# A hybrid GLA and Fourier layer on one core: modulation loads issued by GpSimd, folds a step further ahead, no VectorE modulation in the output gates

## The chip, the cores and the metric

The kernel runs on one core of one Trainium2 chip. The metric is the device time of one execution in microseconds, as the median of several runs. The core has five engines that work in parallel, each through its own list of instructions: PE (TensorE, matrix products), ACT (ScalarE), DVE (VectorE), POOL (GpSimd) and SP (SyncE, which here only issues transfers). Semaphores order the engines against each other. Transfers between the chip's memory and the core run on 16 DMA engines.

## What is computed

The reference is one layer of a diffusion backbone for 128 context tokens and 256 latent tokens, with 2048 channels. It is applied to both sets, which share all weights. Cut to what matters here:

```
mod = silu(cond) @ w_ada + b_ada            # 6 x 2048 values for each of 2 conditions
sh1, sc1, ga1, sh2, sc2, ga2 = split(mod, 6)
h = rmsnorm(x) * (1 + sc1) + sh1
q, k, v, g, lr_f, lr_b, fo = split(h @ w_in)
o = gla(q, k, v, decays) ; o = rmsnorm(o) * silu(g)
f = real(fft2(fo))                          # over positions and over 256 channels of a group
g_a, g_b = split(sigmoid(h @ w_gate + b_gate))
m = (g_a * (o @ w_br_gla) + g_b * (f @ w_br_four)) @ w_out
x = x + ga1 * rmsnorm(m)
h = rmsnorm(x) * (1 + sc2) + sh2
x = x + ga2 * rmsnorm((silu(h @ w_ffn_gate) * (h @ w_ffn_up)) @ w_ffn_down)
```

Everything is in float32. The modulation is a product of a 2048 x 12288 matrix with only two vectors, and its six parts of 2048 are wanted at different times: the first two at the start, the third (ga1, m = 2) in the output projection, the fourth and fifth (m = 3 and 4) before the feed-forward part, the last one at the end.

## The kernel before

**Data.** The 384 tokens lie along the free axis, channels along the 128 partitions. A float32 product is made of three matrix products of halves: each operand is split into a high and a low part (`hi`, `lo`), and hi x hi, hi x lo and lo x hi are summed (`gemm`, L311 to L317). A weight arrives as a tile `raw` of 128 x 1024; ACT copies its high part (L275, L281) and DVE subtracts it for the low part (L276, L282). All weights are listed in the order of use in `srcs` (L158 to L214). `load` (L218) takes the next one with a transfer issued by SP, `split` makes the two parts, and `grab` hands out the next finished pair and pushes another one in, so that about three pairs stand ready. `proj` (L335) makes 128 output channels ("a unit") from h in two half units of 24 matmuls each, and after each half unit calls `step(side)`, which advances a generator of side work by one step. The orders of PE, ACT, DVE and POOL are those in which the program writes its instructions; SP's order is made by a scheduler.

**Modulation.** There are two ways to sum a half of one part (16 tiles of 128 x 1024, 512 KB each). `ada_gemv` (L685) has PE do it: one load (L690) and eight small matmuls (L692; printed as one line of x8) at each step. `ada_rest` (L661) has DVE do it: one load (L666) and two DVE operations (L669 for the first tile, L671 for the others) at each step, then eight matmuls with a selecting matrix (L679) that bring the sums together. Both end in `ada_tail` (L643): ACT copies the sum (L645), PE transposes it (L649), DVE adds the bias and writes `mods`. All loads share two buffers, `adaw`. DVE's sums run through `paced` (L344), which advances them by `rate` steps for each step of the side work and carries fractions over.

**Stages.** After the start (norm, first modulation, values of the GLA) the program goes through these, and PE's own products set the order in each:

- The GLA stage, with the q and k units, then GF = 26 units of the merge gates. Their side work (L939) advances the scan of the GLA, `gl`, by one step, and one step of modulation: in a cycle of seven, PE's sums (`summed`) at the second and fifth, DVE's (`ada`) at the others. A finished gate is written to memory by SP (`gates_d`, L954).
- The fold stage, with the remaining gate units in `turns` half units. The Fourier transform over positions uses that cosines are even and sines odd, so h is first folded over the positions: `over_ends` (L700; DVE L702, L707, L708 and ACT L703) adds and subtracts mirrored positions, `over_parts` (L710) splits the result into `hF` (ACT L356, DVE L357), and `across_n` (L981) makes the product of hF with folded weights into four sums (PE L993, L994). The weights of these products are folded too (`fold_across`, DVE L248 and L249). What is done after each half unit is in the table `after` (L166 to L173): `("ends", n)`, `("parts", n)` and `("f", h, n)` for n from 0 to 7, and h from 0 to 1 for the two halves of the Fourier columns. `run_after` (L1003) goes through it. Three spare buffers for raw weights are in use in this stage. It ends with a small product for the Nyquist columns (`pfq`, L1031).
- The output gates and the branches (`mix_order`): eight units of the GLA's output gate with side work of `summed`, `df` (the transform over positions, L1065) and `ada` at rate 0.5, and after each `next(nw)`, which builds small Nyquist weights `wn` from eight transfers of 12 KB (`nyq_weights`, L1114); between them, from the third on, the Fourier units, `four` (L1181), and then the GLA branch units.
- The output projection, `wout` (L1269 on), 16 units, with `ada` at rate 0.8. After unit i = KT - 4 = 12 everything that `ada_gen` still has is drained in one go, since its buffers are needed. Each unit ends in ACT squares (L1266) and DVE sums (L1277, L1281).
- The feed-forward part, which the change leaves as it is.

The pacing and the drain read:

```
def paced(gen, rate):
    due = 0.0
    while True:
        due += rate[0]
        while due >= 1.0:
            due -= 1.0
            if next(gen, 1) is not None:
                return
        yield
...
            if i == KT - 4:
                for _ in ada_gen:
                    pass
```

Of the kernel before, what the change touches and what calls it, by code (L numbers as in the profile page):

```python
# [35 lines left out]
NFC = FT // FC  # L36
G = 1024
XU = 2
GF = 26
BF = 10  # L40
GD = 256

# [65 lines left out]
def tile_step(ctx: ExitStack, tc: tile.TileContext, a, o):  # L108
    nc = tc.nc
    PE, ACT, DVE, POOL, SP = nc.tensor, nc.scalar, nc.vector, nc.gpsimd, nc.sync  # L110
# [54 lines left out]

    turns = 2 * (32 - GF)  # L166
    after = [[] for _ in range(turns)]
    for n in range(8):
        after[n].append(("ends", n))
        after[n + 1] += [("f", 0, n), ("parts", n + 1)]  # L170
    left = turns - 9
    for n in range(8):
        after[9 + n * left // 8].append(("f", 1, n))  # L173
    across = set()
    for at, todo in enumerate(after):
        srcs.append(a["w_gate"][GF + at // 2, at % 2])
# [484 lines left out]
    def ada_rest(todo):  # L661
        for m, half in todo:
            acc = adap.tile([P, 2, 1024], F32, tag="adacc", name="adacc")
            for k in range(KT):
                w = adap.tile([P, 1024], F32, tag="adaw", name="adaw", bufs=2)
                SP.dma_start(w, a["w_ada"][m - 2, half, k])  # L666
                for c in range(2):
                    if k == 0:
                        DVE.tensor_scalar_mul(acc[:, c, :], w, spad[:, k, c : c + 1])  # L669
                    else:  # L670
                        DVE.scalar_tensor_tensor(  # L671
                            acc[:, c, :], w, spad[:, k, c : c + 1], acc[:, c, :], op0=ALU.mult, op1=ALU.add,
                        )
                yield
            yield
            pr = pss.tile([P, 256], F32, tag="side", name="pr")
            for c in range(2):
                for j in range(4):
                    PE.matmul(  # L679
                        pr[32 * j : 32 * j + 32, :], selr[:, 32 * c : 32 * c + 32],  # L680
                        acc[:, c, j * 256 : (j + 1) * 256], start=c == 0, stop=c == 1,
                    )
            yield from ada_tail(pr, m, half)

    def ada_gemv(m, half):  # L685

        pr = pss.tile([P, 256], F32, tag="side", name="pr")
        for k in range(KT):
            w = adap.tile([P, 1024], F32, tag="adaw", name="adaw", bufs=2)
            SP.dma_start(w, a["w_ada"][m - 2, half, k])  # L690
            for j in range(4):
                PE.matmul(  # L692
                    pr[32 * j : 32 * j + 32, :], spad[:, k, :], w[:, j * 256 : (j + 1) * 256],
                    start=k == 0, stop=k == KT - 1,
                )
            yield
        yield from ada_tail(pr, m, half)
# [12 lines left out]
    def over_parts(k, r):  # L710

        x = hF[k // 4]
        split_act(*(x[:, k % 4 : k % 4 + 2, n, :] for n in range(2)), r)
# [9 lines left out]
    rate = [1.0]  # L723
    ada_gen = ada_rest([(m, half) for m in (2, 3) for half in range(2)])
    ada = paced(ada_gen, rate)
    with ExitStack() as s:
# [209 lines left out]
        gl = gla()  # L936
        summed = ada_gemv(4, 0)

        def side():  # L939
            while True:  # L940
                for n in range(7):
                    next(gl, None)
                    next(summed if n % 3 == 1 and n < 6 else ada, None)
                    yield

        sd = side()
        for i in qk_order[1:]:
# [17 lines left out]
    parts = ((0, HT, 0), (HT, T, HT + HL))  # L965
    fs = ctx.enter_context(ExitStack())
    px = fs.enter_context(tc.tile_pool(name="px", bufs=1))
    with ExitStack() as s:
# [5 lines left out]
        sums, folds = [], {}  # L974
# [28 lines left out]
        def run_after():  # L1003
            for at, todo in enumerate(after):
                for what, *n in todo:
                    if what == "ends":
                        ends(*n)
                    elif what == "parts":
                        if n[0] in folds:
                            over_parts(2 * n[0], folds.pop(n[0]))  # L1010
                    else:
                        if n[0] == 0 and n[1] in folds:
                            over_parts(2 * n[1], folds.pop(n[1]))
                        if n == [1, 5]:
                            depth[0] = 2
                            spare_raws.clear()
                        across_n(*n)
                yield
# [21 lines left out]
    with ExitStack() as s:  # L1040
# [73 lines left out]
        def nyq_weights():  # L1114

            n = D // 2
            for h in range(2):
                wr = pc.tile([P, n], F32, name="wr")
                POOL.memset(wr, 0.0)
                for g in range(4):  # L1120
                    src = a["w_br_four"][8 * h : 8 * h + 8, 32 * g : 32 * g + 1, (2 * g + 1) * P : (2 * g + 2) * P]
                    SP.dma_start(
                        wr[g : g + 65 : 32, :].rearrange("p (i c) -> p i c", c=P),
                        src.rearrange("i p c -> p i c").to_broadcast([3, 8, P]),
                    )
                    if g % 2:
                        yield
                w = wn[:, n * h : n * h + n]
                ACT.copy(w, wr)
                DVE.tensor_sub(w[32:64], wr[32:64], w[32:64].bitcast(F32))  # L1130
                yield

        df = dft()

        summed = ada_gemv(4, 1)
        rate[0] = 0.5

        def side():
            while True:
                next(summed, None)  # L1140
                next(df, None)
                next(ada, None)
                yield

        sd = side()
        nw = nyq_weights()
        oT = alloc_r("B", "o")

        def gcol(p, i):
# [60 lines left out]
        for b, i in mix_order:  # L1210
            if b == "o":
                if i == 1:
                    gate_of()
                proj(psm, hT, lambda p: gcol(p, i), sd)
                next(nw, None)
                if i == 1:
                    gate_of()
                continue
            if b == "b":
                for g in (df, nw):  # L1220
                    for _ in g:
                        pass
                next(summed, None)
                four(i)
            else:
                if mT is None:
                    mT = alloc_A()
                p = psm.tile([P, T], F32, tag="mm", name="pmm")
                gemm(p, grab(hold=True), oT, 8)
                g, y = gates.pop((b, i))  # L1230
                DVE.tensor_mul(g, g, p)
                DVE.tensor_add(y, y, g)
                settle()
# [13 lines left out]
    with ExitStack() as s:  # L1247
# [42 lines left out]
            ACT.activation(sq2, mg32(i), AF.Square)  # L1290
            return sq0, pr, sq2

        rate[0] = 0.8
        spare_h = {-4: ((pe, "hid_hi", 1), (pe, "hid_lo", 1)), -2: ((pe, "S0", 1), (pe, "S1", 1))}
        spare_w = ((adap, "adaw", 2), (adap, "adaw", 2))
        raw2 = None
        for i in range(KT):
            p = psm.tile([P, T], F32, tag="mm", name="pmm")
            for g in range(2):
                n = 2 * i + g - 2 * KT  # L1300
                if n < -6:
                    w = grab()
                else:

                    w = take()
# [376 lines left out]
        n = 0  # L1682
# [353 lines left out]
```

## Time and profile before

| | us |
|---|---|
| median of 3 runs | 2013.39 (2011.44 to 2013.53) |
| the profiled execution, device time | 2014.74 |
| its span in the trace | 2012.9 |
| mean granted TensorE clock | 0.988 |

The profile is of one execution. A row of the timeline has the start, the length, the engine, the line of the kernel, the operation, its output and inputs, sizes and a count; what stands in square brackets is the idle time of the engine before it and what ended it. Groups by line have count, busy time, mean ns of one and idle time before. A window's row sums the busy time of each engine in a stretch of time. In the wait view a row reads: engine, instruction, what released it, then the sum of the waits in us, how many, and the longest. The stages of the trace are: start to 147, GLA stage from there to 468, fold stage to 584, output gates and branches to 817, wout to about 952, feed-forward to the end.

### The profile page before, as it was taken

Reading aid. Unit: us, or ns where it says so; the run is one execution under the profiler, and the core shown is the slowest. Engines: PE = TensorE matmul, PEld = TensorE weight load, DVE = VectorE, ACT = ScalarE, POOL = GpSimd, SP = SyncE. Lnnn points to the kernel's source line nnn. Section 1 sums busy time; section 2 is a strip of 40 time slices with the busy share of each in tenths; the row PEclk is TensorE's granted clock in tenths of the full one; section 3 lists DMA queues with packets and bytes.
Section 4 is the critical chain, followed back from the end, with each engine's and each line's share of the span. In section 5 each row is a group of like instructions: output and inputs, shape, how many; then the busy total and the mean of one; then the engine's idle time right before and its main releaser. Section 6 shows DMA issues by size and latency. Waiting matters only on the chain.

```text
span 2012.9 us, 27779 instructions
## 1 busy us (share of the span) xinstructions
PE 1955.7 (97%) x10678; PEld 1709.9 (85%) x10678; DVE 1602.1 (80%) x2128; ACT 915.7 (45%) x1298; POOL 33.2 (2%) x55
## 2 busy tenths in 40 slices
PE   8998999997898899999999999999999999999998
PEld 6778999997897799999988888888888888888886
DVE  5666767677755778896878988999999889987886
ACT  4234454543344465445645444444444444444445
POOL 0000000000000000000300000000000000000001
PEclk9998999999899899999999999999999999999999
DMA  9976767775355778665627363635455354626244
GB/s 390 381 248 201 255 202 232 243 225 189 123 175 167 247 240 264 218 200 178 215 84 222 103 204 94 205 118 181 133 176 165 128 185 129 197 87 192 73 143 151
DMA packets 200597, 380.55 MB, mean 189 GB/s; under 512 B 14092, under 2 KB 126924, under 8 KB 196112
## 3 DMA queue, kind: packets, MB, share of 16 engines
q1 hardware_dynamic: 199936, 378.51, 57.7%
q8 instruction: 84, 1.38, 0.3%
q14 instruction: 49, 0.40, 0.1%
q10 hardware_dynamic: 528, 0.26, 0.0%
HBM read 361.94 MB, written 16.78 MB: 188 GB/s over the span
## 4 chain that ended last, share of the span: by engine, by line
PE 70%; DVE 3%; DMA 2%; ACT 1%; issue 1%; POOL 0%; DVEq 0%; ACTq 0%; POOLq 0%
PE pgu L327 29%; PE pdn L327 17%; PE pmm L315 16%; PE pf L1191 2%; PE pfo L993 1%; PE pmm L1453 1%; PE pf L1192 1%; DMA adaw<-in_w_ada 1%; PE ptr L1745 1%; PE pr L692 1%; PE pfo L994 0%; DMA raw<-in_w_d 0%; DVE x1b L1897 0%; DVE wlo L1611 0%; ACT hF L356 0%
## 5 line engine op out<-in xcount | busy, mean ns | idle before, releaser
L315 PE MATMUL pmm<-A_hi,whi 128*128 128x384 f32 x1072 | 365.1, 341 | 0.0
L315 PE MATMUL pmm<-A_lo,whi 128*128 128x384 f32 x1072 | 360.1, 336 | 0.0
L315 PE MATMUL pmm<-A_hi,wlo 128*128 128x384 f32 x1072 | 360.0, 336 | 0.0
L1600 ACT CAST whi<-u 128x1024 fp32r<-128x1024 f32 x200 | 210.6, 1053 | 273.3 <-DVE u L1584 86.2
L276 DVE TENSOR_TENSOR wlo<-raw,whi 128x1024 fp32r<-128x1024 f32 x163 | 198.6, 1221 | 103.5 <-ACT whi L275 102.1
L1600 ACT CAST whi<-raw 128x1024 fp32r<-128x1024 f32 x175 | 184.2, 1053 | 211.2 <-DMA raw<-in_w_g 69.6
L1611 DVE TENSOR_TENSOR wlo<-u,whi 128x1024 fp32r<-128x1024 f32 x200 | 243.8, 1219 | 28.7 <-ACT whi L1600 18.7
L327 PE MATMUL pgu<-whi,A_hi 128*128 128x512 f32 x640 | 250.0, 391 | 0.0
L327 PE MATMUL pgu<-whi,A_lo 128*128 128x512 f32 x640 | 249.3, 389 | 0.0
L275 ACT CAST whi<-raw 128x1024 fp32r<-128x1024 f32 x165 | 172.9, 1050 | 149.7 <-DMA raw<-in_w_out 65.0
L1611 DVE TENSOR_TENSOR wlo<-raw,whi 128x1024 fp32r<-128x1024 f32 x175 | 213.3, 1219 | 34.4 <-ACT whi L1600 24.8
L315 PEld LDWEIGHTS pmm<-A_hi,whi 128*128 128x128 f32 x1072 | 202.6, 189 | 10.9 <-issue 9.3
L315 PEld LDWEIGHTS pmm<-A_lo,whi 128*128 128x128 f32 x1072 | 202.7, 189 | 0.2
L315 PEld LDWEIGHTS pmm<-A_hi,wlo 128*128 128x128 f32 x1072 | 202.4, 189 | 0.0
L327 PE MATMUL pdn<-whi,hid_hi 128*128 128x512 f32 x480 | 187.0, 390 | 1.1 <-ACT psums L1760 1.1
L327 PE MATMUL pdn<-whi,hid_lo 128*128 128x512 f32 x480 | 186.8, 389 | 0.0
L327 PE MATMUL pgu<-wlo,A_hi 128*128 128x512 f32 x640 | 184.2, 389 | 0.0
L671 DVE SCALAR_TENSOR_TENSOR adacc<-adaw,spad,adacc 128x1024 f32<-128x1024 f32 x120 | 148.5, 1278 | 0.8 <-DMA adaw<-in_w_ada 0.7
L327 PEld LDWEIGHTS pgu<-whi,A_hi 128*128 128x128 f32 x640 | 120.1, 188 | 26.1 <-issue 0.8
L327 PEld LDWEIGHTS pgu<-wlo,A_hi 128*128 128x128 f32 x640 | 120.2, 188 | 25.4
L327 PEld LDWEIGHTS pgu<-whi,A_lo 128*128 128x128 f32 x640 | 120.2, 188 | 25.0
L327 PE MATMUL pgu<-whi,S 128*128 128x512 f32 x480 | 131.1, 395 | 0.0
(402 smaller groups left out, 3019.9 us busy)
## 6 DMA issues: line engine op xcount, KB each, us to landing
adaw<-in_w_ada SPq DMA_DIRECT2D x96, 512.0 KB, 4.3
raw<-in_w_d SPq DMA_DIRECT2D x88, 512.0 KB, 4.1
slab<-in_w_ada SPq DMA_DIRECT2D x32, 1024.0 KB, 10.6
raw<-in_w_gate SPq DMA_DIRECT2D x64, 512.0 KB, 4.6
raw<-in_w_g SPq DMA_DIRECT2D x48, 512.0 KB, 4.1
raw<-in_w_u SPq DMA_DIRECT2D x48, 512.0 KB, 3.7
raw<-in_w_in SPq DMA_DIRECT2D x44, 512.0 KB, 4.7
u<-in_w_u SPq DMA_DIRECT2D x40, 512.0 KB, 4.6
```

The source lines that it names most:

```text
L275: ACT.copy(hi, raw)
L276: sub = lambda: eng.tensor_sub(lo, raw, hi.bitcast(F32))
L315: PE.matmul(dst, w[wi][:, k * n + n0 : k * n + n0 + P], x[xi][:, k0 + k, :], start=first and k == 0 and j == 0, stop=last and k == kts - 1 ...
L327: PE.matmul(dst, stat[x_][m], mov(w[w_], m), start=first and w_ == m == x_ == 0, stop=last and w_ == m == 1,)
L671: DVE.scalar_tensor_tensor(acc[:, c, :], w, spad[:, k, c : c + 1], acc[:, c, :], op0=ALU.mult, op1=ALU.add,)
L692: PE.matmul(pr[32 * j : 32 * j + 32, :], spad[:, k, :], w[:, j * 256 : (j + 1) * 256], start=k == 0, stop=k == KT - 1,)
L993: PE.matmul(p, w_of[0][:, i, k, g, :], x[:, :, lo:hi], start=kt == 0, stop=False)
L1191: PE.matmul(pf[:, 0 : 2 * HT], w[0][:, c], x[k], start=k == 0, stop=False)
L1192: PE.matmul(pf[:, 0:HT], w[1][:, c], x[k][:, 0:HT], start=False, stop=m == 1 and k == 3)
L1453: PE.matmul(hp[u], hw[u][j][:, ((k - 1) % 8) * P : ((k - 1) % 8 + 1) * P], h2[m][:, k - 1, :], start=k == 1 and j == m == 0, stop=k == KT ...
L1600: ACT.copy(hi, src)
L1611: DVE.tensor_sub(lo, src, hi.bitcast(F32))
```

## The change

Seven edits, all in the stages from the GLA to wout:

- the loads of both modulation sums and the eight Nyquist loads are issued by POOL instead of SP;
- GF is 25 instead of 26, so that one more gate unit, two half units, stands in the fold stage (14 turns instead of 12);
- in the table of the fold stage, the split of a fold (`parts`) and its product (`f`) stand one and two turns behind the fold (`ends`), at the head of their turn, where the product stood one turn behind, with the split directly before it; the second half's products begin at turn 10 and spread over the turns that are left;
- in the GLA stage PE's modulation sums stand at the third and sixth step of each cycle of seven, in every cycle, and the cycle is counted through;
- in the output gates the side work has no `ada` step any more, and the Nyquist weights' steps move into it, from once a unit to once a half unit;
- rate 0.5 for the output gates falls away, and the rate in wout is 0.82 instead of 0.8;
- in the Nyquist weights, the two yields stand behind the four loads instead of between them.

```diff
-GF = 26
+GF = 25
...
-        after[n + 1] += [("f", 0, n), ("parts", n + 1)]
-    left = turns - 9
+        after[n + 1].insert(0, ("parts", n))
+        after[n + 2].insert(0, ("f", 0, n))
     for n in range(8):
-        after[9 + n * left // 8].append(("f", 1, n))
+        after[10 + n * (turns - 10) // 8].append(("f", 1, n))
...
                 w = adap.tile([P, 1024], F32, tag="adaw", name="adaw", bufs=2)
-                SP.dma_start(w, a["w_ada"][m - 2, half, k])
+                POOL.dma_start(w, a["w_ada"][m - 2, half, k])
...
         def side():
+            n = 0
             while True:
-                for n in range(7):
-                    next(gl, None)
-                    next(summed if n % 3 == 1 and n < 6 else ada, None)
-                    yield
+                next(gl, None)
+                next(summed if n % 7 in (2, 5) else ada, None)
+                n += 1
+                yield
...
                     elif what == "parts":
-                        if n[0] in folds:
-                            over_parts(2 * n[0], folds.pop(n[0]))
+                        over_parts(2 * n[0], folds.pop(n[0]))
                     else:
-                        if n[0] == 0 and n[1] in folds:
-                            over_parts(2 * n[1], folds.pop(n[1]))
...
-                    SP.dma_start(
+                    POOL.dma_start(
                         wr[g : g + 65 : 32, :].rearrange("p (i c) -> p i c", c=P),
                         src.rearrange("i p c -> p i c").to_broadcast([3, 8, P]),
                     )
-                    if g % 2:
-                        yield
+                yield
+                yield
...
         summed = ada_gemv(4, 1)
-        rate[0] = 0.5
+        nw = nyq_weights()
 
         def side():
             while True:
                 next(summed, None)
                 next(df, None)
-                next(ada, None)
+                next(nw, None)
                 yield
...
                 proj(psm, hT, lambda p: gcol(p, i), sd)
-                next(nw, None)
...
-        rate[0] = 0.8
+        rate[0] = 0.82
```

The load of `ada_gemv` changes in the same way as the one shown.

More of the change, by code (lines that the diff above doesn't have):

```diff
@@ L689, in ada_gemv @@
             w = adap.tile([P, 1024], F32, tag="adaw", name="adaw", bufs=2)
-            SP.dma_start(w, a["w_ada"][m - 2, half, k])
+            POOL.dma_start(w, a["w_ada"][m - 2, half, k])
             for j in range(4):
@@ L1141, in side @@
                 next(df, None)
-                next(ada, None)
+                next(nw, None)
                 yield
         sd = side()
-        nw = nyq_weights()
         oT = alloc_r("B", "o")
```

## The prediction

> **What bounds the kernel now.** I read the page's head and its table of DMA issues, then the windows by stage, then the waits of PE and SP.
>
> ```profile
> span 2012.9 us, 27779 instructions
> PE 1955.7 (97%) x10678; PEld 1709.9 (85%) x10678; DVE 1602.1 (80%) x2128; ACT 915.7 (45%) x1298; POOL 33.2 (2%) x55
> adaw<-in_w_ada SPq DMA_DIRECT2D x96, 512.0 KB, 4.3
> ```
>
> TensorE is busy for 97% of the span: a change can win only part of the 57 us in which PE idles, and it loses whatever new idling it makes. The span lies within a profiled execution of 2014.74 us. The 96 transfers of the last row (4.3 us from issue to landing) are the modulation loads that move from SP to GpSimd; how long one takes there is the first unknown, L below. The windows are the start of the GLA stage, the fold stage, most of the output-gate stage, and wout up to its modulation's end (columns: window and length, then busy time and count of PE, PEld, DVE, ACT, POOL, then the granted clock, the DMA share and GB/s):
>
> ```profile
> 147.00:219.00 72.00, 65.64 (x400) 62.05 (x400) 52.23 (x65) 29.79 (x44) 0.62 (x2) 0.93 0.66 218
> 474.00:584.50 110.50, 91.89 (x574) 88.07 (x573) 78.08 (x114) 44.51 (x74) 0.24 (x2) 0.92 0.47 152
> 632.00:726.00 94.00, 81.70 (x506) 74.25 (x503) 62.58 (x113) 45.38 (x65) 0.96 (x1) 0.89 0.64 209
> 817.00:940.00 123.00, 123.00 (x722) 122.10 (x721) 104.86 (x129) 59.38 (x97) 0.00 (x0) 1.00 0.62 204
> ```
>
> PE idles 6.4 us in the first, 18.6 in the fold stage, 12.3 in the output gates, nothing in wout. In wout the clock is full and PE never waits, but DVE is busy for 104.86 of 123 us: there is nothing to win there, and little room.
>
> ```profile
> PE pr L692 <- DMA adaw<-in_w_ada: 17.2, 5, 5.3
> PE pfo L993 <- DVE hF L357: 16.1, 7, 8.8
> SPq L666 <- DVE adacc L671: 108.3, 36, 9.4
> ```
>
> Two waits make most of PE's idle time: 17.2 us in five waits for modulation loads, 16.1 in seven for folds of h. SP's 108.3 us behind DVE look larger, but they lie where PE is full (wout is one such place), so moving them off SP's queue is worth nothing there.
>
> **The change part by part. Wout: loads that arrive too late to be spread.** Without the output gates' share, wout must sum 23 modulation loads on DVE where it summed 16. Rate 0.82 brings 19 of them up to unit 12; in the built order the last four stand in one burst, and directly behind them, before unit 13's matmuls, PE has L679, which waits for the burst.
>
> ```profile
> 895.31 0.49 ACT L1266 ACTIVATE sq<-pmm 128x384 f32<-128x384 f32 x1
> 900.97 2.47 DVE L671 SCALAR_TENSOR_TENSOR adacc<-adaw,spad,adacc 128x1024 f32<-128x1024 f32 x2
> 919.39 0.49 ACT L1266 ACTIVATE sq<-pmm 128x384 f32<-128x384 f32 x1 [0.34 <-PE pmm L315]
> 905.35 1.07 PE L679 MATMUL pr<-adacc,selr 128*32 128x256 f32 x16
> 909.15 0.36 ACT L645 COPY adev<-pr 128x256 f32<-128x256 f32 x1
> 463.16 0.38 PE L649 MATMUL ptm<-ident,adev 128*128 128x128 f32 x2
> 650.09 1.08 PE L692 MATMUL pr<-adaw,spad 128*32 128x256 f32 x8 [3.93 <-DMA adaw<-in_w_ada]
> 655.64 0.64 PE L692 MATMUL pr<-adaw,spad 128*32 128x256 f32 x8
> 651.10 0.69 PE L1191 MATMUL pf<-edT,whi 128*128 128x388 f32 x1
> 656.21 0.45 PE L1191 MATMUL pf<-edT,whi 128*128 128x388 f32 x1
> 658.71 0.36 PE L315 MATMUL pmm<-A_hi,whi 128*128 128x384 f32 x1
> ```
>
> Seven more loads are 7 x 2.47 = 17.3 us of DVE: 104.9 + 17.3 = 122 of 123. DVE therefore runs late up to unit 12, as it already did at unit 9, where the modulation pair ends at 903.44, 8.1 us after the square that its unit's matmuls released (895.31). So, with T the end of unit 12's matmuls (about 919.1), the last paced pair ends at T + 8.1, the first pair of the burst (its load is there) at T + 10.5. Only two buffers exist: the load of the second was let go at T + 8.1, lands at 8.1 + L and is summed by 10.5 + L; the third rides beside it; the fourth's goes out when the second is summed, and ends at 12.9 + 2L. Then L679 (1.07 hot; 2.1 at the slow clock that follows idling), the copy and its handoff 0.7, the transposes 0.5, and a slow first stretch. That stretch is 2.0 us: a Fourier unit took 4.54 us (651.10 to 655.64) straight after a stall and 2.50 (656.21 to 658.71) later. The 1.4 us of these that PE paid before, without waiting, come off: a loss of 16.8 + 2L. Nothing hides it: all matmuls behind L679 wait in PE's order.
>
> **How long a load takes from GpSimd.** No row of before shows one.
>
> ```profile
> DMA to landing us min/median/max: 3.5/4.0/5.2
> raw<-in_w_v SPq DMA_DIRECT2D x16, 512.0 KB, 6.7
> ```
>
> The first row (loads of L690) gives 3.5 as the lower bound, the second, the same size amid a loaded start, 6.7 as the upper. I take 5.3, next to the slowest of L690's (5.2) and one microsecond over the 4.3 of the ninety-six: the queue is another, untried in this trace, and an issue that GpSimd has to work for is likelier to add time than to save it. The loss in wout is then 27.4 us (23.8 to 30.2).
>
> By the Trainium skill (DMA: Bandwidth & Descriptors, "Anatomy of one DMA — SWDGE (gpsimd) path") a GpSimd transfer takes about 2.0 us plus its bytes at 436 GB/s; that is an estimate of 3.2 us here, below every row of SP, and the loss would be 23.2. No run here shows it yet.
>
> **Output gates: the gain.**
>
> ```profile
> 627.08 0.64 PE L692 MATMUL pr<-adaw,spad 128*32 128x256 f32 x8
> 627.78 5.38 SPq L690 DMA_DIRECT2D adaw<-in_w_ada  x3
> 631.30 1.01 PE L692 MATMUL pr<-adaw,spad 128*32 128x256 f32 x8 [3.58 <-DMA adaw<-in_w_ada]
> 674.23 1.08 PE L692 MATMUL pr<-adaw,spad 128*32 128x256 f32 x8 [5.32 <-DMA adaw<-in_w_ada]
> 584.25 0.26 POOL L1060 MEMSET nyq<- 128x192 f32 x1 [113.38 <-PE pfq L1031]
> 588.43 0.64 PE L692 MATMUL pr<-adaw,spad 128*32 128x256 f32 x8
> ```
>
> A load for DVE sat in one of the two buffers, so the second of two close steps could start its load only when PE had finished the first (627.08 + 0.64, issue 627.78, use 631.30). Three such stalls, 3.58 + 3.93 + 5.32 = 12.8 us, and about 2.1 us of slow clock after each, 6.3. Without DVE's loads both buffers serve PE. What remains comes from the built order: loads 11 and 15 are let go one step and one Fourier unit ahead (0.64 + 2.50 = 3.15 us), loads 10 and 14 some 5.25 ahead. The first load is queued on POOL behind the clearing of nyq, which waits for PE: out at 584.5, wanted at 588.43, 3.9 us. At L = 5.3 these stall 2 x 2.15 + 0.05 + 1.4 = 5.75, with about 2.1 of slow clock. Gain: 12.8 + 6.3 - 5.75 - 2.1 = 11.3 (18.4 at 3.5, 14.4 at 4.3, nothing at 6.7). The eight small Nyquist loads also go to POOL's queue; two steps of at least 4 us each cover them, and DVE's removed work lay in idle time.
>
> **Fold stage: a small gain.**
>
> ```profile
> 459.19 0.58 ACT L953 ACTIVATE gz<-pmm,bgate 128x384 f32<-128x384 f32 x1 [3.28 <-PE pmm L315]
> 467.97 0.57 ACT L953 ACTIVATE gz<-pmm,bgate 128x384 f32<-128x384 f32 x1
> L276 DVE TENSOR_TENSOR wlo<-raw,whi 128x1024 fp32r<-128x1024 f32 x163 | 198.6, 1221 | 103.5 <-ACT whi L275 102.1
> 475.80 1.04 ACT L275 CAST whi<-raw 128x1024 fp32r<-128x1024 f32 x1 [7.26 <-issue]
> 484.88 0.69 PE L993 MATMUL pfo<-hF,whi 128*128 128x388 f32 x1 [8.82 <-DVE hF L357]
> 495.53 0.95 DVE L702 TENSOR_TENSOR t<-A_hi,A_lo 128x768 f32<-128x768 f32 x1
> 492.38 0.96 DVE L357 TENSOR_TENSOR hF<-r,hF 128x768 fp32r<-128x768 f32 x1 [1.90 <-ACT hF L356]
> 504.67 0.95 DVE L702 TENSOR_TENSOR t<-A_hi,A_lo 128x768 f32<-128x768 f32 x1
> 547.93 0.45 PE L993 MATMUL pfo<-hF,whi 128*128 128x388 f32 x1 [0.23 <-DVE hF L357]
> 581.33 1.99 PE L1031 MATMUL pfq<-hF,wq 128*4 128x194 f32 x44
> ```
>
> Units end every 8.78 us (gz rows), half a unit is 4.39. With 25 units ahead of it the stage opens at 459.2, not 468.0, and gets two half units more, so PE's work is the same. One turn of DVE takes 9.14 us (495.53 to 504.67; over the first product's seven turns (547.93 - 484.88)/7 = 9.0), PE's half unit and product only about 6.7: DVE sets the pace. The built order shows each turn with the same DVE and ACT instructions in the same sequence; only PE's product stands a turn later, and its weights' low part now ends the same DVE turn that held hF. So the pace stays; only start and end move. The first spare weight still arrives 7.8 us after the last gz (475.80 - 467.97), since its buffer opens with the stage. From there the first product stood 9.1 us off (475.80 to 484.88); the fold of h no longer waits behind a gate weight on DVE (L276, 1.2) and a gz on ACT (0.57), which leaves 7.3. So it comes 15.1 after the opening instead of 16.9. The second follows after a turn less one L276, 7.8, the eighth six turns later: 15.1 + 7.8 + 6 x 9.0 = 76.9, at 536.1. Then come the 33.4 us of before (547.93 to 581.33) and one half unit more: 573.9 against 581.33 is 7.4 us gained; with turns of 8.8 it is 9. I take 9 (5 to 13, by the start and the turns).
>
> **GLA start.** The five L692 waits sum to 17.2; 12.8 are told above, 4.4 stood at this start with some 2 of slow clock. The new cycle puts those steps third and sixth of seven. One stall of about 3 to 5 remains, so near nothing, less about a microsecond later where SP's loads had little slack: -1 (-3 to +3).
>
> **Sum.** -27.4 + 11.3 + 9 - 1 = -8.1, so 2022.8 for the profiled execution. That execution is 1.35 above the median of runs: 2021.5.
>
> **Rivals.** *Faster: the fold stage loses DVE's wait.* For: turns hold 1.90 us of DVE waiting for ACT's hF, and the product is now a turn later, so something might refill the gap. Against: the chain from the folded weights over ACT's casts to L357 is unchanged. Price: 7 x 1.9 = 13 more, so -8.1 + 13 = +5, 2008.5. It decides once a turn falls below about 7.9 us. *Short landing, 3.5:* -23.8 + 18.4 + 9 + 1 = +4.6, 2008.8; for it, the fastest L690 rows, and a queue of its own; the equation quoted from the Trainium skill would lead here. *Landing as on SP, 4.3:* -25.4 + 14.4 + 9 + 0 = -2.0, 2015.4: no change. *Slow GpSimd path, 6.7:* -30.2 + 0 + 9 - 3 = -24.2, 2037.6; for it, one POOL queue that serves 104 loads in order beside a busy DVE.
>
> ```profile
> L669 DVE TENSOR_SCALAR adacc<-adaw,spad x8: 744/747/749, 152.0 to 822.7; 128x1024 f32<-128x1024 f32 x8
> ```
>
> The Trainium skill (SBUF — State Buffer, "SBUF: two separate sides") speaks against this change: GpSimd cannot write descriptors while DVE runs in a mode that takes both port pairs. Of the DVE operations quoted only L669 has a time that looks like it (0.75 us against 2.47 / 2 = 1.24 for L671), and it runs eight times in all, so by the trace that rule adds little to the slow case.
>
> **How the numbers follow.** Forecast 0.45; slow path 0.16; landing as on SP 0.16; the two faster cases 0.12 (short landing) and 0.11 (fold). About 4 us (0.2%) separates change from no change in this measurement. Slower holds the first two: 0.61; same 0.16; faster 0.23. The range is 2006 to 2036, from inside the faster pair to just short of the slow case; the forecast alone has 2017.5 to 2028.
>
> **What would show it.** The table of DMA issues shows L itself, in a row of POOL's queue. Right in wout: three or more L671 pairs in a row near 910 to 930 with gaps of DVE waiting for adaw, and one PE wait of 20 us or more before L679, with PE below 105 of 123. Right in the output gates: L692 waits of about 2 us in pairs instead of 3.6 to 5.3. Right in the fold stage: turns still near 9 us, seven waits of L993 now naming wlo, pfq near 573. I am wrong if wout's wait is under 15 us (DVE kept up, or unit 13 did not stand behind L679), or if the fold's turns shorten.

## The result, and the profile after

| | before | after |
|---|---|---|
| median of 12 runs, us | 2013.45 (2011.44 to 2015.82) | 2020.05 (2015.3 to 2021.87) |
| ratio to before, 95% interval | | 1.003 (1.0021 to 1.0039) |
| profiled execution, us | 2014.74 | 2020.2 |
| its span, us | 2012.9 | 2018.3 |

The change makes the kernel 6.6 us slower; 2021.5 had been forecast. The page of the changed kernel, its head and the first row of its table of transfers:

```profile
span 2018.3 us, 27813 instructions
PE 1951.9 (97%) x10678; PEld 1706.3 (85%) x10678; DVE 1602.8 (79%) x2128; ACT 914.6 (45%) x1298; POOL 89.1 (4%) x159
adaw<-in_w_ada POOLq DMA_DIRECT2D x96, 512.0 KB, 4.4
```

A load takes 4.4 us from GpSimd, against 4.3 from SP. The busy time of PE, DVE and ACT is what it was, within 4 us; POOL's grows from 33.2 to 89.1 us, as it now issues the loads. So the loss is to be looked for in waits. The same windows by stage, shifted with the stages, and the wait view of PE:

```profile
147.00:219.00 72.00, 67.50 (x426) 64.62 (x425) 55.12 (x72) 33.13 (x51) 7.13 (x14) 0.98 0.66 229
460.00:575.00 115.00, 106.27 (x653) 101.66 (x651) 82.92 (x119) 48.03 (x82) 4.63 (x8) 0.94 0.53 167
632.00:715.00 83.00, 76.12 (x480) 72.08 (x481) 57.09 (x116) 44.30 (x66) 4.02 (x8) 0.96 0.70 235
817.00:940.00 123.00, 101.25 (x591) 98.31 (x590) 100.94 (x121) 46.94 (x77) 8.97 (x17) 0.90 0.60 197
```

```profile
PE pr L679 <- DVE adacc L671: 21.1, 1, 21.1
PE pr L692 <- DMA adaw<-in_w_ada: 9.9, 5, 3.3
...
PE pfo L994 <- DVE hF L357: 3.3, 3, 1.3
PE pfo L995 <- DVE wlo L282: 2.8, 6, 0.7
```

PE idles 4.5 us in the first window instead of 6.4, 8.7 instead of 18.6 in the fold stage, 6.9 instead of 12.3 in the output gates, and 21.8 instead of nothing in wout. The old two waits have shrunk from 17.2 to 9.9 and from 16.1 to some 6 us; one new wait of 21.1 takes that back and more.

To see where the difference grows, the same events are placed in time in each profiled execution (from rows of ACT and PE; "gz 1" is the first finished gate unit, "L649" the end of the output gates' modulation, the squares are those of wout's units, the last row but one is the end of SP's last row of output transfers, which is the last issue there and not the landing):

| us in the span | before | after | difference | step |
|---|---|---|---|---|
| gz 1 | 218.75 | 214.56 | -4.2 | -4.2 GLA start |
| gz 25 | 459.19 | 454.94 | -4.3 | 0 |
| pfq | 581.33 | 566.58 | -14.8 | -10.5 fold stage |
| L649 | 695.45 | 670.59 | -24.9 | -10.1 output gates |
| square of unit 1 | 826.41 | 803.98 | -22.4 | +2.4 branches |
| square of unit 12 | 919.39 | 895.59 | -23.8 | -1.4 |
| square of unit 13 | 927.71 | 929.51 | +1.8 | +25.6 wout |
| last output row ends | 2008.21 | 2009.42 | +1.2 | -0.6 |
| end of span | 2012.9 | 2018.3 | +5.4 | +4.2 end of program |

The rows behind the wout step, from the timelines of ACT, DVE, POOL and PE of the changed kernel:

```profile
895.59 0.49 ACT L1262 ACTIVATE sq<-pmm 128x384 f32<-128x384 f32 x1
901.77 4.87 DVE L671 SCALAR_TENSOR_TENSOR adacc<-adaw,spad,adacc 128x1024 f32<-128x1024 f32 x4
904.54 0.53 POOL L666 DMA_DIRECT2D adaw<-in_w_ada  x1 [5.00 <-DVE adacc L671]
908.50 4.92 DVE L671 SCALAR_TENSOR_TENSOR adacc<-adaw,spad,adacc 128x1024 f32<-128x1024 f32 x4 [1.86 <-DMA adaw<-in_w_ada]
911.27 0.53 POOL L666 DMA_DIRECT2D adaw<-in_w_ada  x1 [3.81 <-DVE adacc L671]
915.35 2.48 DVE L671 SCALAR_TENSOR_TENSOR adacc<-adaw,spad,adacc 128x1024 f32<-128x1024 f32 x2 [1.93 <-DMA adaw<-in_w_ada]
916.69 2.28 PE L679 MATMUL pr<-adacc,selr 128*32 128x256 f32 x16 [21.14 <-DVE adacc L671]
919.46 0.69 PE L649 MATMUL ptm<-ident,adev 128*128 128x128 f32 x2 [0.49 <-ACT adev L645]
919.80 0.67 PE L315 MATMUL pmm<-A_hi,whi 128*128 128x384 f32 x1
```

PE ends unit 12 at about 895.5 and waits until 916.69, as all its next matmuls stand behind L679. Five pairs of L671 stand in a row, with two gaps of 1.9 us in which DVE waits for a load that could start only when a buffer came free (issue 904.54 for the pair at 908.50, issue 911.27 for the one at 915.35). Then the matmuls run at the slow clock, 2.28 us where they took 1.07.

### The profile page after: what moved, and what is told of

The parts are those of the page before. It is cut to its first block, busy times and chain, and to the rows that moved or that the text cites. A ratio compares the mean times of both kernels' runs of the same rounds, so it can differ in the third digit from the quotient of the medians.

```text
span 2018.3 us, 27813 instructions
## 1 busy us (share of the span) xinstructions
PE 1951.9 (97%) x10678; PEld 1706.3 (85%) x10678; DVE 1602.8 (79%) x2128; ACT 914.6 (45%) x1298; POOL 89.1 (4%) x159
## 4 chain that ended last, share of the span: by engine, by line
PE 78%; DMA 8%; DVE 7%; issue 5%; ACT 2%; POOL 0%; SPq 0%; DVEq 0%; ACTq 0%; POOLq 0%
PE pgu L327 28%; PE pmm L315 21%; PE pdn L327 17%; PE pv L469 3%; DMA adaw<-in_w_ada 3%; DMA raw<-in_w_br_gla 2%; PE pgm L452 1%; DVE wlo L276 1%; DMA raw<-in_w_out 1%; PE pmm L1449 1%; PE pfo L994 1%; DVE adacc L671 1%; DVE wlo L1607 1%; PE pr L692 1%; ACT whi L275 1%
## 5 line engine op out<-in xcount | busy, mean ns | idle before, releaser
L276 DVE TENSOR_TENSOR wlo<-raw,whi 128x1024 fp32r<-128x1024 f32 x163 | 198.8, 1221 | 94.5 <-ACT whi L275 94.4
L671 DVE SCALAR_TENSOR_TENSOR adacc<-adaw,spad,adacc 128x1024 f32<-128x1024 f32 x120 | 148.4, 1279 | 5.2 <-DMA adaw<-in_w_ada 5.0
L327 PEld LDWEIGHTS pgu<-wlo,A_hi 128*128 128x128 f32 x640 | 120.1, 188 | 25.4
```

Of the source, the lines that this page charges most:

```text
L276: sub = lambda: eng.tensor_sub(lo, raw, hi.bitcast(F32))
L327: PE.matmul(dst, stat[x_][m], mov(w[w_], m), start=first and w_ == m == x_ == 0, stop=last and w_ == m == 1,)
L671: DVE.scalar_tensor_tensor(acc[:, c, :], w, spad[:, k, c : c + 1], acc[:, c, :], op0=ALU.mult, op1=ALU.add,)
```

## Experiments

Each run is one kernel on the chip with a profile, timed in rounds against the kernel before; ratios are to that kernel. "Before" stood at 2012.3 to 2013.5 us in these comparisons.

**Loads back on SP.** The changed kernel with all 104 loads on SP; the other two places in the code change in the same way as the one shown.

```diff
-                POOL.dma_start(w, a["w_ada"][m - 2, half, k])
+                SP.dma_start(w, a["w_ada"][m - 2, half, k])
```

> The changed kernel with all its modulation and Nyquist loads issued by SP again, nothing else undone. Theory: GpSimd's queue costs about 4 us after the last output transfer (the span of the changed kernel ends 5.2 us after its data stops, before 1.3) and nothing else, since its loads land in 4.4 us as SP's do in 4.3: so 2016, with the 21 us wait before L679 still there. Rival one: the queue is also what won 4.3 us in the GLA stage: then 2020, no change against the changed kernel. Rival two: without its own queue the loads come late again in the output gates, and those stalls return: 2022 or more.

Measured: 2007.71 us, ratio 0.9973 (0.9963 to 0.9984). Without GpSimd's loads the rest of the change is a gain of 5.8 us; the queue costs 12.3 us, not 4. The theory had one part right, the 4 us at the end, and missed the rest; neither rival held: the queue won nothing in the GLA stage (gz 1 at 212.72, earlier still), and the output gates took 104.1 us from pfq to L649 as with GpSimd (104.0). Of the 12.3 us 4.2 lie at the program's end. In wout unit 12 to unit 13 takes 30.8 us against 33.9:

```profile
PE pr L679 <- DVE adacc L671: 17.2, 1, 17.2
```

Another 4.1 us lie between the end of the output gates and unit 1 of wout (-25.4 to -27.1 on SP, -24.9 to -22.4 on GpSimd). The two profiled executions are 10.4 us apart, the medians 12.3; the other stages differ by 1 to 2 us either way, within the scatter told below. Why the branch units suffer is not settled. One wait of PE for DVE (1.25 us, at 792.95) is part of it, and so is the granted clock from 670 to 720, 0.94 with GpSimd's loads and 0.97 with SP's (an estimate of 1.5 us); no run takes the rest apart.

**GpSimd loads alone,** all 104, in the kernel before; again one of three like places is shown.

```diff
-                SP.dma_start(w, a["w_ada"][m - 2, half, k])
+                POOL.dma_start(w, a["w_ada"][m - 2, half, k])
```

> The kernel before with its modulation and Nyquist loads issued by GpSimd, nothing else. Theory: +4 us at the end of the program, the stalls of the output gates about as before (a load of DVE still sits between two close steps), GLA stage as before: 2017. Rival: the queue is what won the GLA stage 4.3 us: 2013.

Measured: 2030.94 us, ratio 1.0095 (1.008 to 1.011): 17.5 us slower. The theory and the rival both forecast too little, and the gain that the rival expected in the GLA stage did not come (gz 1 at 218.75, as before). The output gates took 126.7 us instead of 114.1. POOL's timeline and one row of PE's in that run:

```profile
634.46 0.95 POOL L1119 MEMSET wr<- 128x1024 f32 x1 [11.40 <-DVE wn L1130]
635.70 2.30 POOL L1122 DMA_DIRECT2D wr<-in_w_br_four  x4 [0.29 <-POOL wr L1119]
637.99 1.15 POOL L690 DMA_DIRECT2D adaw<-in_w_ada  x2
641.97 1.08 PE L692 MATMUL pr<-adaw,spad 128*32 128x256 f32 x8 [12.62 <-DMA adaw<-in_w_ada]
```

The second clearing of `wr` waits 11.4 us for DVE to be done with the first half of the Nyquist weights. POOL takes its list in order, so two modulation loads that are ready stand behind it, with four small issues in between (2.30 us), and PE waits 12.62 us for the first of them. The landing itself took 4 us (637.99 to 641.97). The same step waited 3.58 us in the kernel before (the row at 631.30), so 9 us of the 12.6 that the output gates lost are this wait's. In the changed kernel the same clearing comes earlier, and its loads are not yet wanted:

```profile
600.09 0.95 POOL L1117 MEMSET wr<- 128x1024 f32 x1 [12.94 <-DVE wn L1128]
601.34 2.30 POOL L1120 DMA_DIRECT2D wr<-in_w_br_four  x4 [0.29 <-POOL wr L1117]
603.63 1.15 POOL L690 DMA_DIRECT2D adaw<-in_w_ada  x2
```

What moved the clearing is the new place of the Nyquist steps, in the side work of the half units. The version told below that has DVE's sums back in the gates, with GpSimd's loads and this new place, shows that it does not take the removal of the sums: the same step waits 4.30 us there, not 12.62.

```profile
621.56 1.08 PE L692 MATMUL pr<-adaw,spad 128*32 128x256 f32 x8 [4.30 <-DMA adaw<-in_w_ada]
```

So this move, which the prediction had treated as neutral, keeps GpSimd's loads from costing some 9 us more there.

**Nyquist loads alone on GpSimd,** eight of 12 KB, in the kernel before.

```diff
-                    SP.dma_start(
+                    POOL.dma_start(
                         wr[g : g + 65 : 32, :].rearrange("p (i c) -> p i c", c=P),
```

> The kernel before with only the eight 12 KB Nyquist loads issued by GpSimd. Theory: the end of the program takes 4.2 us longer as soon as any load goes through GpSimd's queue, however few: last output issue to end of span 8.9 instead of 4.7 us, time 2017. Rival: the end grows with the number of such loads (104 in the changed kernel): then less than 1 us, 2013 to 2014.

Measured: 2011.79 us, ratio 0.9993 (0.9984 to 1.0003). The rival holds. SP's last row of outputs before, after, and here, and the packets of GpSimd's queue after and here (views of queues):

```profile
1996.77 11.44 SPq L1901 DMA_DIRECT2D out_yT<-x1b  x11
```

```profile
1998.01 11.41 SPq L1897 DMA_DIRECT2D out_yT<-x1b  x11
...
q0 software_dynamic: 14080, 50.44, 7.9%
```

```profile
1993.33 11.43 SPq L1901 DMA_DIRECT2D out_yT<-x1b  x11
...
q0 software_dynamic: 256, 0.10, 0.0%
```

From the end of that row to the end of the span there are 4.7 us before (2012.9 - 2008.2), 5.0 here (2009.8 - 2004.8) and 8.9 after (2018.3 - 2009.4). The end grows by 0.3 us with 8 loads and by 4.2 with 104: about 0.04 us for each load. Of the two counts that differ, it goes with the loads (13 times as many) and not with the packets (55 times as many). The four versions with 104 such loads have 8.9 us there, and the nine with none 4.6 to 4.7.

**The fold stage alone:** new table and GF = 25 in the kernel before.

```diff
-GF = 26
+GF = 25
...
-        after[n + 1] += [("f", 0, n), ("parts", n + 1)]
+        after[n + 1].insert(0, ("parts", n))
+        after[n + 2].insert(0, ("f", 0, n))
...
```

The second half's turns and `run_after` change with it, as in the whole change.

> The kernel before with the new table of the fold stage and GF = 25 alone; all loads on SP, old cycle, old output gates. Theory: the fold stage's gain of 10.5 us belongs to these two edits: 2003. Rival: the first spare weight came early only because SP's queue was free of modulation loads, and with them back the first product stands 3 to 5 us later: 2006 to 2008.

Measured: 2014.02 us, ratio 1.0005 (0.9995 to 1.0014). The stage's gain is there but small, as the rival had it: from the 25th gate unit to pfq it takes 116.9 us, before 122.1, in the changed kernel 111.6. DVE's first fold of a weight and PE's first product in this run, then DVE's in the changed kernel:

```profile
468.67 0.69 DVE L248 TENSOR_TENSOR raw<-raw 128x512 f32<-128x512 f32 x1 [6.07 <-DMA raw<-in_w_in]
...
475.35 0.69 PE L993 MATMUL pfo<-hF,whi 128*128 128x388 f32 x1 [5.30 <-DVE hF L357]
```

```profile
461.67 0.69 DVE L248 TENSOR_TENSOR raw<-raw 128x512 f32<-128x512 f32 x1 [3.69 <-DMA raw<-in_w_in]
```

The first spare weight comes 11.3 us after the opening (457.36, the 25th gate unit) here and 6.7 after it (454.94) in the changed kernel. The rival's reason is only half of it: the version with loads on SP needs 112.9 us for the stage, nearly the changed kernel's, so it is not SP's queue as such. SP's rows in the fold part alone:

```profile
461.01 0.33 SPq L690 DMA_DIRECT2D adaw<-in_w_ada  x1
463.34 0.38 SPq L227 DMA_DIRECT2D raw<-in_w_in  x1
```

A modulation load that waits for a sum of DVE (L671, until 460.98) stands in front of the first spare weight, which so goes out 6.0 us after the opening. The version with loads on SP has the new GLA cycle; there the same kind of load goes out at 454.56, 1.5 us after the opening (453.11), and the weight 2.6 us after it, as in the changed kernel. What the rival did not say is that the 7.1 us that PE was ahead at pfq (1.8 of them from the GLA stage's scatter) were lost again but for 0.9 us: 3.3 in the output gates, 1.8 by the end of the last Fourier unit, 1.2 by the square of wout's first unit. One part is a wait of 2.1 us for a raw weight (at 584.05), where PE arrived earlier at a load that did not; the rest is not taken apart.

**The GLA cycle alone,** in the kernel before.

```diff
-                for n in range(7):
-                    next(gl, None)
-                    next(summed if n % 3 == 1 and n < 6 else ada, None)
-                    yield
+                next(gl, None)
+                next(summed if n % 7 in (2, 5) else ada, None)
+                n += 1
+                yield
```

> The kernel before with the new cycle of the GLA stage alone (PE's sums at the third and sixth step of seven). Theory: this is where the changed kernel gained 4.3 us by the end of the first gate unit (214.6 against 218.8 us): one stall less, so the first gate unit ends at 213 to 215 and the time is 2008 to 2010. Rival: the gain there is the scatter of one stall from execution to execution (the version with the fold part alone, which has the old cycle, ended it at 216.9): first gate unit at 217 to 219, time 2013.

Measured: 2007.98 us, ratio 0.9974 (0.996 to 0.9987). The theory holds. The PE rows of L692 that waited at the start of the GLA stage, before and here:

```profile
163.54 0.88 PE L692 MATMUL pr<-adaw,spad 128*32 128x256 f32 x8 [0.48 <-DMA adaw<-in_w_ada]
182.26 1.08 PE L692 MATMUL pr<-adaw,spad 128*32 128x256 f32 x8 [3.85 <-DMA adaw<-in_w_ada]
```

```profile
168.98 1.08 PE L692 MATMUL pr<-adaw,spad 128*32 128x256 f32 x8 [2.87 <-DMA adaw<-in_w_ada]
```

Two stalls became one. All five profiled executions with the old cycle have a long wait of 3.9 to 5.7 us near 182; the nine with the new one have in its place one of 1.0 to 3.0 near 170. The clock granted from 147 to 212 is 0.92 to 0.95 in the five and 0.97 to 1.00 in the nine. The five with the old cycle end gate unit 1 at 216.9 to 218.8 us, the nine at 212.3 to 215.0: there is scatter of 2 to 3 us, but the groups do not meet. This is the cheapest part of the change and brings 5 us by itself.

**The output gates alone,** with loads on SP: no DVE sums there, the Nyquist steps moved, rate 0.82. The yields of the Nyquist weights and the old call of `next(nw)` change too, as in the whole change, and are left out here.

```diff
-        rate[0] = 0.5
+        nw = nyq_weights()
...
-                next(ada, None)
+                next(nw, None)
...
-        rate[0] = 0.8
+        rate[0] = 0.82
```

> The kernel before with the edits of the output gates alone: no DVE sums there, Nyquist steps in the side work, rate 0.82 in wout, all loads on SP. Theory: this edit by itself moves a loss, gates 11 us shorter, unit 12 of wout 22.5 us longer (what the version with loads on SP shows, 30.8 instead of 8.3 us from unit 12 to unit 13): 2013 + 11.5 = 2025. Rival: the gain in the gates belongs partly to the stage's earlier start in the changed kernel and is only 5 here: 2030.

Measured: 2014.59 us, ratio 1.0008 (0.9998 to 1.0019). Theory and rival both forecast too much time. The edit does move a loss, but the sum is near nothing: the gates gain 15.8 us (98.3 instead of 114.1 from pfq to L649; the long stalls are gone), and wout loses 19.0:

```profile
645.08 0.64 PE L692 MATMUL pr<-adaw,spad 128*32 128x256 f32 x8 [1.24 <-DMA adaw<-in_w_ada]
...
663.21 0.64 PE L692 MATMUL pr<-adaw,spad 128*32 128x256 f32 x8 [1.13 <-DMA adaw<-in_w_ada]
...
915.70 2.28 PE L679 MATMUL pr<-adacc,selr 128*32 128x256 f32 x16 [14.49 <-DVE adacc L671]
```

**Sums back in the gates.** The changed kernel with DVE's sums in the output gates again, first with GpSimd's loads, then with SP's.

```diff
+        rate[0] = 0.5
...
                 next(nw, None)
+                next(ada, None)
...
-        rate[0] = 0.82
+        rate[0] = 0.8
```

> The changed kernel with DVE's sums back in the output gates (rate 0.5 there, 0.8 in wout), loads still on GpSimd. Theory: the two sides of that edit are separate, so the wait of 21 us before L679 goes, with its restart (25 us in all), and the stalls of the output gates return, some 10 us: 2020 - 25 + 10 = 2005. Rival: with both kinds of loads in GpSimd's one queue behind the Nyquist clearing, the gates lose 20 us or more, as the version with GpSimd loads alone did (12 us over the kernel before): 2015 or more.

> The changed kernel with DVE's sums back in the output gates and with all loads on SP: what is left of the change is the fold stage and the GLA cycle. Theory: their gains add up, 3 to 5 us of the cycle and 5 to 9 of the fold stage, less the 3 that the output gates gave back with the fold part alone: 2003 (2000 to 2006). Rival: the output gates give everything back, as the fold part alone ended at no change: 2010.

Measured: 2014.04 us with GpSimd, ratio 1.0009 (0.9996 to 1.0022), and 2005.23 with SP, ratio 0.9962 (0.9951 to 0.9973). With SP the theory holds: cycle and fold stage together, with the Nyquist steps in their new place, bring 7 to 8 us. With GpSimd the profiled execution (2009.1) lay well under the median of runs that went from 2009 to 2021, so for this version only the sign is clear: the wait before L679 goes, three stalls of 4.2 to 4.3 us return to the gates, and the sum is some 4 to 6 us under the changed kernel, not 15.

**Wout at rate 1.0,** in the changed kernel, and the same with loads on SP.

```diff
-        rate[0] = 0.82
+        rate[0] = 1.0
```

> The changed kernel with rate 1.0 in wout instead of 0.82, so that two loads go with each unit and no burst is left after unit 12. Theory: of the 25 us lost there most is the chain of two loads in series and the restart, while DVE itself has 114 us of work for the 108 us of thirteen units: PE then waits some 8 us, and the time is near 2003. Rival: DVE is full, and what it cannot do in time only moves into waits of the units for their low parts: 2016 to 2020.

> The changed kernel with loads on SP and rate 1.0 in wout. Theory: the two corrections are independent, 12.3 us for the queue and 13.1 for the spread burst (less the 3 us by which the burst is shorter on SP): 2020 - 12.3 - 13.1 + 3.1 = 1998. Rival: with the loads on SP DVE still sets the pace in wout and weights queue behind modulation loads that wait for it: 2003 or more.

Measured: 2006.88 us, ratio 0.9973 (0.9962 to 0.9984), and 1995.27 with SP, ratio 0.9913 (0.9892 to 0.9934). One number moves 13 us. From the square of unit 1 to that of unit 13 it takes 109.2 us, where before took 101.3 and the changed kernel 125.5: the 8 us that were expected from DVE's load remain, and the time of the first is between its theory (2003) and its rival, nearer the theory. PE's wait and the window of wout of the first of the two:

```profile
PE pr L679 <- DVE adacc L671: 4.8, 1, 4.8
```

```profile
804.00:910.00 106.00, 100.61 (x588) 97.66 (x587) 102.17 (x122) 44.43 (x74) 10.56 (x20) 0.97 0.66 227
```

DVE is busy for 102.2 of 106 us: now it is full, and the rest of the loss is its work. With SP's loads the two corrections add up, a little better than expected.

**Sums in the branch units,** with loads on SP: eight of DVE's sums spread over the sixteen GLA branch units, and then four over the last eight, with rate 0.95 in wout.

```diff
+        rate[0] = 0.5
...
                 DVE.tensor_add(y, y, g)
                 settle()
+                next(ada, None)
```

> The changed kernel with its loads on SP, and with eight of DVE's modulation sums moved out of wout into the branch units that follow the output gates (one step at rate 0.5 in each of the sixteen GLA branch units). Theory: DVE has 23 us to spare between 685 and 802 us, so the eight sums (20 us) cost nothing there, and the 22 us that the version with loads on SP still loses behind unit 12 are gone: 2007.7 - 22 = 1986. Rival: the branch units need DVE for their gated sums, and the sums in front of them delay those: some 10 us come back, 1996 or more.

> The changed kernel with loads on SP, four of DVE's sums in the last eight GLA branch units (rate 0.5 there), where fewer Fourier units stand between, and rate 0.95 in wout. Theory: DVE then has about 104 us of work for the 108 us of thirteen wout units, and the branch units lose 1 to 3 us instead of the 9 of eight sums: 1990. Rival: any sum in the branch units costs its own 2.5 us and wout stays bound by DVE: 1995 to 1998.

In the second the added step stands under `if i >= 8:`. Measured: 1995.51 us for eight, ratio 0.9909 (0.9893 to 0.9926), and 1988.81 for four late ones, ratio 0.9882 (0.9863 to 0.9901). Eight sums take the wait out of wout, but the branch units lose 9.3 us (from -26.0 at L649 to -16.7 at unit 1), as the rival had it; PE's rows there show four waits of 0.63 us for the low part of a weight, and one for a Fourier unit's sums:

```profile
719.97 0.45 PE L315 MATMUL pmm<-o_hi,whi 128*128 128x384 f32 x1 [1.57 <-DVE fd L1194]
729.37 0.36 PE L1190 MATMUL pf<-edT,wlo 128*128 128x194 f32 x1 [0.63 <-DVE wlo L276]
```

The 23 us that the expectation gave DVE in that stretch are what the changed kernel leaves (93.4 of 117 us busy); in the version with loads on SP it is busy for 98.3 of the 117, so 18.7 were free for eight sums of 2.5. With them DVE is busy for 43.7 of 45 us from 720 to 765, where Fourier units stand. Four later sums come with a loss of 3.4 us (-30.1 to -26.7), 3.2 of it one wait for DVE at 788.66, and wout has no stall left, with DVE at 95.3 of 105:

```profile
797.00:902.00 105.00, 105.00 (x627) 103.27 (x626) 95.25 (x115) 44.59 (x74) 0.00 (x0) 1.00 0.68 217
```

The theory (1990) holds. This version is faster than both kernels: 23.5 us under before, some 30 under the changed one.

## Why the prediction was right, and where it was not

The time, its sign and the main cause were right; several terms had errors that cancel, and one cost was not seen.

| term, us (a loss is positive) | predicted | measured |
|---|---|---|
| wout's burst | +27.4 | +25.6 |
| output gates | -11.3 | -10.1 |
| fold stage | -9 | -10.5 |
| GLA stage | +1 | -4.2 |
| branches and up to unit 12 | 0 | +1.0 |
| end of program and the rest | 0 | +3.6 |
| sum | +8.1 | +5.4 |

That the forecast lay 1.5 us from the median is partly luck. Three terms came out better than forecast, by 8.5 us together, and three worse, by 5.8. And the landing was taken too long: with the measured 4.4 us the prediction's own sums give +25.6 for wout, -14.0 for the gates and +2.6 in all. That is 2016, and less than the 4 us that the prediction asked of a change.

- **Wout.** The mechanism held step by step: four loads left over, two buffers, loads in series, L679 directly behind unit 12. "16.8 + 2L" gives 24.8 with the 4.0 us that the loads of the burst took (904.54 to 908.50, 911.27 to 915.35), and 25.6 were measured. Only L was mis-sized, 5.3 for 4.4 overall (with 4.4 the formula gives 25.6). The choice among the nearest rows should have been the median of the same transfer from SP. The estimate from the Trainium skill's equation (DMA: Bandwidth & Descriptors, "Anatomy of one DMA — SWDGE (gpsimd) path"), 3.2 us, was lower than any load here: 3.7 is the shortest.
- **What GpSimd costs.** This is the step that failed, though the sum hides it. The prediction priced the move by the landing alone, and the landing is as good as on SP. By the profiled executions, 10.4 us apart, what the queue costs in this kernel lies at the program's end (4.2), in the burst (3.1) and around the branch units (4.1, mechanism in part open), less 1.0 elsewhere. The kernel before with GpSimd's loads shows a further price, a wait of 12.6 us, some 9 more than on SP, behind a clearing in POOL's order. The prediction had seen that pattern for the first load only: there it gave 1.4 us and 3.3 were measured, as that load took 7.0 us to land (570.02 to 577.01).
- **Output gates.** The three stalls became three of 0.5 to 2.6 us (3.8 together) and that first one (3.3). At the measured landing the formula had 2.5 and 0.5, and these 4.1 us are the difference between its 14.0 and the 10.1 measured. Alone, the same edit won 15.8; with SP's loads the changed kernel's gates are as long as with GpSimd's, so that difference is not the queue's, and it stays open.
- **Fold stage.** DVE's pace held (60.8 us from first to eighth product, 8.7 a turn; 9.0 before), and the first product stood 13.4 us after the opening, not 15.1. The reason given for that step was wrong, though: a gate weight on DVE (L276 at 466.20) and a gz on ACT (465.12) still stand ahead of hF. What is earlier is the raw weight, 6.7 us after the opening instead of 7.8, and it is now the folded one, so DVE need not finish another weight before it begins to fold h: that is 1.3 us behind the weight instead of 2.2, and from there to the product it takes 5.3 us instead of 6.9. That the waits would name `wlo` was right for six; three still name hF. The experiment adds what was not foreseen: without the new cycle half of this gain goes, and what is left is given back later.
- **GLA stage.** Wrong in sign. The prediction expected one stall of 3 to 5 us to be worth the two it replaces, and a microsecond lost later. The stall is 2.80 us, and its eight matmuls take 0.64 us (the row at 169.87) where those behind the long stall of before took 1.08. The clock granted in the first window is 0.98 instead of 0.93, and nothing is lost later (-4.2 at gz 1 and -4.3 at gz 25).
- **The rivals.** The fold stage kept DVE's wait. The case "as on SP" had the landing right and the time wrong by 3.4 us in the profiled execution: it lacked the 4.2 us at the end of the program and gave the gates 4.3 too much, and it missed the 4.2 of the GLA stage the other way. The slow path did not come: the longest landing was 9.1 us, and the median 4.5 for L690.

Rows of the landings in the changed kernel, for L690 and for L666:

```profile
DMA to landing us min/median/max: 3.7/4.5/9.1
```

```profile
DMA to landing us min/median/max: 3.7/4.4/7.0
```

The stall that is left in the GLA stage, and the first load of the output gates with its use:

```profile
169.87 0.64 PE L692 MATMUL pr<-adaw,spad 128*32 128x256 f32 x8 [2.80 <-DMA adaw<-in_w_ada]
...
570.02 0.53 POOL L690 DMA_DIRECT2D adaw<-in_w_ada  x1 [0.21 <-issue]
577.01 0.70 PE L692 MATMUL pr<-adaw,spad 128*32 128x256 f32 x8 [3.26 <-DMA adaw<-in_w_ada]
```

The rows of DVE and ACT in front of the changed kernel's first product:

```profile
465.07 1.22 DVE L282 TENSOR_TENSOR wlo<-raw,whi 128x1024 fp32r<-128x1024 f32 x1
466.20 1.22 DVE L276 TENSOR_TENSOR wlo<-raw,whi 128x1024 fp32r<-128x1024 f32 x1
467.34 0.95 DVE L357 TENSOR_TENSOR hF<-r,hF 128x768 fp32r<-128x768 f32 x1
```

```profile
465.12 0.58 ACT L954 ACTIVATE gz<-pmm,bgate 128x384 f32<-128x384 f32 x1
```

## What to carry to other kernels

Work that is paced through a stage with a rate must be counted to its end: what the rate does not bring in time is done in one burst, without cover, at the place where its result is wanted, and one number (0.82 to 1.0) was worth 13 us here. Before loads move to another engine's queue, look at what else that engine does in order: the landing time can stay the same while a clearing in front of a load costs some 9 us. And when an edit gains in one stage, follow the gain to the end of the program: the fold stage's gain alone was lost again, but for 0.9 us, by the first unit of wout, one part of it where PE met a load that came no earlier.

## What was not expected of the hardware

The end of the program grows with the number of loads that were issued by GpSimd, though the last of them had landed more than a thousand microseconds earlier (last issue at 911.27, the end at 2018.3): 4.7 us from the last output row to the end of the span with none, 5.0 with 8, 8.9 with 104. The output itself is not later for it: from 2011 to 2013 the DMA engines are busy for 0.23 of the time before and for 0.85 after, so by this the last bytes move some 3.3 us behind that row in both, and the rest of the time they stand still. What the chip does in that time no row shows.
